# Moving a scan, a square and the splits of pooled rows on two vector engines of a hybrid encoder layer

## The chip, the cores and the metric

The kernel runs on one core of one Trainium2 chip. A core has a matrix engine (TensorE, PE in the profile; its weight loads are shown as PEld), a vector engine (VectorE, DVE), an activation engine (ScalarE, ACT), a general engine (GpSimd, POOL) and a queue for transfers (SyncE, SP). Each engine works through its own list of instructions in order, and semaphores tie the lists together. The metric is the device time of the whole kernel in microseconds, taken as the median of several runs.

## What is computed

One layer for 512 tokens of width 1024, all in fp32. The input is normalised and projected to the columns of three token mixers and of three gates; the mixers' results are projected, gated and added, projected once more and added to the input; a gated feed-forward block follows.

```
h = rms_norm(x);  u_pool, u_lru, q, k, v, g = split(h @ w_in)
y_pool[g] = (mean of the last w tokens of u_pool[g] - u_pool[g]) @ w_pool[g] * scale    w = 2, 4, 8, 16
y_lru     = scan h_t = a_t * h_(t-1) + b_t,   a, b from a conv and two block gates of u_lru
y_sb      = stick-breaking attention, 8 heads x 128; q and k are RMS-normed by head:
            q * rsqrt(mean(q^2)),  k * rsqrt(mean(k^2))
merged = sum over mixers of sigmoid(g_m) * (y_m @ w_branch[m])
x = x + merged @ w_out;   x = x + (silu(h2 @ w_fg) * (h2 @ w_fu)) @ w_fd
```

## The kernel before

**Products in three parts.** Every fp32 operand of a large matmul is split into a high part in a reduced format (float32r) and a low part, the rest. A product is then three matmuls: high by high, high by low, low by high (`mm3`). Weights come from HBM as 128x1024 tiles and are split on the chip by `split_w` (lines 131 to 141): ACT copies the tile to `whi` (L139), DVE subtracts that from the tile to give `wlo` (L140). Each of the two tags has three buffers, so the third tile ahead can be split only when PE is done with the oldest. A splitter's two instructions have a high priority (60 above their surroundings), and the weights are asked for some tiles ahead of their use.

**What sets the order.** The program is written as one stream of matmuls. Other work is put into lists of small functions: `bg` (background) and, during attention, `abg`. After each group of matmuls `tick()` takes one entry from `abg` and one from `bg` (two while `bg` has over eight entries), and what these functions write stands there in the program. A scheduler then places each engine's instructions by data and by priority. `tc.issue_after(i)` adds one more rule to what is written inside it: on the engine of `i` it stands behind `i`, with no other wait.

**v, k and q.** The projection for v, k and q (in this order, `VKQ`; t = 2, 1, 0) uses seven products per matrix instead of eight, in the order `11, 12, S2, S1, S3, S4, 22`. `tok_product` does one of them: two weight tiles, 12 matmuls of 512 columns each per tile, with the token blocks (names such as hT3h, hT3l) as the stationary operand and the weight tile as the moving one. Results gather in PSUM. `snap` copies a partial result from PSUM to a buffer `r` on ACT (L841, a high priority), `final` adds another partial result on DVE (L845) and puts `post` into `bg`. For q, `post` squares the block on ACT (L788), adds the squares up by head on DVE (L789) and stores the block by a transfer from POOL. For k, `post2` also scales the block by eight short ACT instructions (L807).

**The recurrence.** The RG-LRU part works in four chunks of 256 channels. Its last steps stand in `bg` behind v's product S3: the input of chunk 3, two scans of chunk 2 and two of chunk 3 (`lru_scan`, L711, one instruction per 128 channels), and the stores. They run beside v's product S4 and 22 and beside k's first products.

**Pooling and attention.** Behind the gates, four pool chunks are projected (`pool_chunk`, order 1, 0, 3, 2), two blocks `j` of 128 channels each. `evac_u` copies a block out of PSUM (ACT L975, tile `up`), `pool_mean` forms the running mean by scans and two more DVE instructions (L985, L986, L987, L989; for window 2 an add), and ends with `split_hl`: ACT copies the block to `p..h` (L932), DVE subtracts to get `p..l` (L933); the name p30h is the high part of chunk 3, block 0. `pool_back` multiplies the blocks by the chunk's small matrix (PSUM tile `pps`) one chunk later. Attention runs from `abg` beside this, a head every five ticks: `trans` transposes q and k on PE (PSUM tile `pq`, L1053), `scores` (L1086 to L1092), `wtrans` transposes the weights (PSUM tile `pw`, L1103) and splits them on ACT (`wth`, L1105, three instructions) and DVE (`wtl`, L1106, three instructions), `yout` multiplies by v. The PSUM tiles pq, pps, pw and py share three buffers, so PE can write the next pq only when the split of an earlier pw has read it.

**The branch products** of the recurrence follow (`ps_br`). Their operands yHH and yHL are loaded from DRAM by POOL (L1192) into the buffers that the normalised input had, once PE has left these. Weights and small tiles are loaded by SP.

Of the kernel before, what the change touches and what calls it, by code (L numbers as in the profile page):

```python
# [8 lines left out]
F32 = mybir.dt.float32  # L9
F32R = mybir.dt.float32r  # L10
BF16 = mybir.dt.bfloat16
AF = mybir.ActivationFunctionType
ALU = mybir.AluOpType
# [51 lines left out]
def layer_kernel(ctx: ExitStack, tc: tile.TileContext, x, xt, vecs, w_in, w_qkv7, w_gate7, w_pool, w_rg, w_ig,  # L65
                 w_branch, w_br7, w_out, w_fg, w_fu, w_fd, w_fd7, out):
    nc = tc.nc
    act = nc.scalar.activation
# [30 lines left out]
    def in_order(ap, b=H):  # L99
        w = ap.ndim == 3  # L100
        if b == H:
            return ap.rearrange("p w (b a) -> p w a b" if w else "p (b a) -> p a b", b=b)
        return ap.rearrange("p (c b a) -> p c a b", a=2, b=b)

    def two(ap, b=H):
        w = ap.ndim == 3
        if b == H:
            return ap.rearrange("p w (a b) -> p w a b" if w else "p (a b) -> p a b", b=b)
        return ap.rearrange("p (c a b) -> p c a b", a=2, b=b)
# [18 lines left out]
    def weight_tiles(nh, nl):  # L128
        return [wp.tile([P, 1024], F32R, tag=tag, name=n)
                for tag, n in (("whi", nh), ("wlo", nl))]  # L130

    def split_w(raw, shape, n):
        hi, lo = weight_tiles("whi" + n, "wlo" + n)
        if len(shape) == 3:
            hi, lo = (t.rearrange("p (a b) -> p a b", a=shape[1]) for t in (hi, lo))
        else:
            hi, lo = (t.rearrange("p (a b c) -> p a b c", a=shape[1], b=shape[2]) for t in (hi, lo))
        with tc.high_priority(60):
            act(hi, raw, AF.Copy)  # L139
            dve.tensor_tensor(lo, raw, hi.bitcast(F32), ALU.subtract)  # L140
        return hi, lo

    def add_direct(key, src, a, b):
# [291 lines left out]
    with ExitStack() as first:  # L435
# [271 lines left out]
        def lru_scan(c):  # L707
            t, s_ = lru[c]["t"], lru[c]["s"]
            h = lru[c]["i"]
            for j in range(2):  # L710
                dve.tensor_tensor_scan(h[:, j, :], t[:, j, :], s_[:, j, :], 0.0, ALU.mult, ALU.add)  # L711
            lru[c] = h
# [39 lines left out]
        def step(*fs):  # L752
            bg.append(lambda: [f() for f in fs])

        def of(f, c):
            return lambda: f(c)
# [27 lines left out]
        def post(t, i, j, r):  # L784
            if t < 2:
                sq = b4([2, 512], f"sq{t}{i}{j}")
                if t == 0:
                    act(sq, r, AF.Square)  # L788
                    dve.tensor_reduce(qss[:, 2 * j:2 * j + 2, 4 * i:4 * i + 4],  # L789
                                      sq.rearrange("p a (b d) -> p a b d", d=HD), AX.X, ALU.add)  # L790
                    store(t, i, j, r)
                    return
                s_ = cst.tile([P, 8], F32, tag="ssq", name=f"ssq{t}{i}{j}", bufs=2)
                act(sq, r, AF.Square)
                dve.tensor_reduce(s_, sq.rearrange("p a (b d) -> p (a b) d", d=HD), AX.X, ALU.add)
                dve.tensor_scalar(s_, s_, 1.0 / HD, EPS, ALU.mult, ALU.add)
                bg.append(lambda: post2(t, i, j, r, s_))
            if t == 2:
                store(t, i, j, r)
# [33 lines left out]
        for t in VKQ:  # L833
            ps = {}
            r = {}


            def snap(key, src):
                r[key] = b4([2, 512], f"r{t}{key[0]}{key[1]}")
                with tc.high_priority(EARLY):  # L840
                    act(two(r[key]), in_order(src), AF.Copy, scale=-1.0 if key[0] else 1.0)  # L841

            def final(key, src):
                v = two(r[key])
                dve.tensor_tensor(v, v, in_order(src), ALU.subtract if key[0] else ALU.add)  # L845
                bg.append(lambda t=t, key=key, v=r[key]: post(t, *key, v))

            def bank(nm):
                ps[nm] = pb.tile([P, 2, 512], F32, tag="mm", name=f"ps_q{t}{nm}")
                return ps[nm]  # L850

            for nm in ORDER:
                if nm in ("11", "12", "S1", "22"):
                    bank(nm)
                dst = {"S2": "11", "S3": "11", "S4": "S1"}.get(nm, nm)
                tok_product(t, nm, ps[dst], dst == nm)
                if nm == "11":
                    snap((0, 0), ps["11"])
                elif nm == "12":
                    final((0, 0), ps["12"])  # L860
                elif nm == "S2":
                    snap((0, 1), ps["11"])
                elif nm == "S1":
                    snap((1, 1), ps["S1"])
                elif nm == "S3":
                    final((1, 1), ps["11"])
                    snap((1, 0), ps["11"])
                elif nm == "S4":
                    final((0, 1), ps["S1"])
                else:  # L870
                    final((1, 0), ps["22"])
                if (t, nm) == (VKQ[0], "S3"):
                    for f, c in ((lru_input, 3), (lru_scan, 2), (lru_scan, 3), (lru_store, 2), (lru_store, 3)):
                        step(of(f, c))


        def gate_done(cc, j, t, ps):
# [51 lines left out]
    def split_hl(src, nm):  # L929
        h = slot_r(nm + "h")  # L930
        l = slot_r(nm + "l")
        act(h, src, AF.Copy)  # L932
        dve.tensor_tensor(l, src, h.bitcast(F32), ALU.subtract)  # L933
        return h, l

    with ExitStack() as mix:
# [41 lines left out]
        def pool_mean(g, j, u):  # L978
            w = 2 << g
            prev = slot(f"pw{g}{j}")  # L980
            if w == 2:
                dve.tensor_copy(prev[:, 0:1], u[:, 0:1])
                dve.tensor_tensor(prev[:, 1:], u[:, 1:], u[:, 0:S - 1], ALU.add)
            else:
                dve.tensor_tensor_scan(prev[:, 0:w], u[:, 0:w], ahead[:, 0:w], 0.0, ALU.add, ALU.add)  # L985
                dve.tensor_tensor_scan(prev[:, w:], u[:, w:], u[:, 0:S - w], prev[:, w - 1:w], ALU.add, ALU.subtract)  # L986
            dve.scalar_tensor_tensor(prev[:, 0:w - 1], prev[:, 0:w - 1], float(w),  # L987
                                     invpos[:, 0:w - 1], ALU.mult, ALU.mult)
            dve.scalar_tensor_tensor(u, prev, 1.0 / w, u, ALU.mult, ALU.subtract)  # L989
            pool_p.setdefault(g, []).append(split_hl(u, f"p{g}{j}"))  # L990

        def pool_back(g, j):
            wh, wl = pool_w[g]
# [12 lines left out]
        def queue_pool_back(g):  # L1006
            for j in range(2):
                bg.append(lambda j=j: pool_back(g, j))
            if g == POOL[1]:
                bg.append(lambda: load_pool_weights(1))  # L1010

        def pool_chunk(g):
            pss = chan_chunk(("pool", g), hn, 1)
            us = [evac_u(pss[j], f"up{g}{j}", g == POOL[3]) for j in range(2)]
            for j in range(2):
                bg.append(lambda j=j, u=us[j]: pool_mean(g, j, u))
            if g != POOL[0]:
                queue_pool_back(POOL[POOL.index(g) - 1])


        def gate_load(br, c):
# [710 lines left out]
```

## Time and profile before

| | us |
|---|---|
| median of 3 runs | 870.37 (870.13 to 870.64) |
| the profiled execution | 870.05 |
| its span in the trace | 868.3 |
| PE busy / weight loads busy | 859.3 / 789.9 |
| DVE busy | 736.4 |
| ACT busy | 522.3 |
| POOL busy | 91.0 |

The granted clock of TensorE was 1.00 over the whole span. The profiled execution is 0.32 us below the median of the runs and 1.75 us above its own span. Times in the trace are counted from the start of the span. In a row of a timeline the columns are start, busy time, engine, line, operation, output and inputs, shapes, count of instructions put together in the row, and in brackets the time that the engine stood idle just before, with what ended it. PE's matmuls are pipelined: in an undisturbed stretch one of 512 columns starts every 0.2155 us (162.60 to 162.82, 353.58 to 353.80), though each is listed with 0.38 us, so a stall is read from the starts: the distance of two starts less 0.2155.

### The profile page before, as it was taken

Reading aid. Unit: us, or ns where it says so; the run is one execution under the profiler, and the core shown is the slowest. Engines: PE = TensorE matmul, PEld = TensorE weight load, DVE = VectorE, ACT = ScalarE, POOL = GpSimd, SP = SyncE. Lnnn points to the kernel's source line nnn. Section 1 sums busy time; section 2 is a strip of 40 time slices with the busy share of each in tenths; the row PEclk is TensorE's granted clock in tenths of the full one; section 3 lists DMA queues with packets and bytes.
Section 4 is the critical chain, followed back from the end, with each engine's and each line's share of the span. In section 5 each row is a group of like instructions: output and inputs, shape, how many; then the busy total and the mean of one; then the engine's idle time right before and its main releaser. Section 6 shows DMA issues by size and latency. Waiting matters only on the chain.

```text
span 868.3 us, 14234 instructions
## 1 busy us (share of the span) xinstructions
PE 859.3 (99%) x5563; PEld 789.9 (91%) x5563; DVE 736.4 (85%) x937; ACT 522.3 (60%) x727; POOL 91.0 (10%) x130
## 2 busy tenths in 40 slices
PE   9999999999999999999999999999999999999998
PEld 7888878888899988889889998889999999999998
DVE  7899897998796698967898786699998888899974
ACT  6554989557866567555665545464555555755642
POOL 1110002232433101000001100000000000021200
PEclk9999999999999999999999999999999999999999
DMA  9586356899592776735736955345543433798913
GB/s 340 168 295 193 98 169 187 226 314 253 178 298 73 240 221 207 228 112 158 217 98 154 211 170 171 98 135 155 153 116 97 114 106 117 225 243 203 196 40 122
DMA packets 116643, 154.08 MB, mean 177 GB/s; under 512 B 8160, under 2 KB 90080, under 8 KB 116576
## 3 DMA queue, kind: packets, MB, share of 16 engines
q1 hardware_dynamic: 103904, 107.30, 38.5%
q0 software_dynamic: 12528, 45.62, 22.3%
q8 instruction: 43, 0.70, 0.3%
q10 hardware_dynamic: 144, 0.26, 0.1%
q14 instruction: 24, 0.20, 0.1%
HBM read 132.71 MB, written 18.87 MB: 175 GB/s over the span
## 4 chain that ended last, share of the span: by engine, by line
PE 56%; DVE 5%; ACT 2%; issue 1%; DMA 1%; SPq 0%; DVEq 0%; ACTq 0%
PE ps_y L313 11%; PE ps_x L313 8%; PE ps_dy L1651 6%; PE ps_dx L1651 5%; PE ps_bY L1276 2%; PE ps_br L305 2%; PE ps_br L304 2%; PE ps_br L306 2%; PE ps_bX L1276 2%; PE ps_out L304 1%; PE ps_out L305 1%; PE ps_out L306 1%; DVE wlo L140 1%; PE ps_fu L306 1%; PE ps_fu L304 1%; PE ps_fu L305 1%
## 5 line engine op out<-in xcount | busy, mean ns | idle before, releaser
L139 ACT ACTIVATE whi<-raw 128x1024 fp32r<-128x1024 f32 x69 | 72.8, 1056 | 72.7 <-PE ps_out L305 15.9
L140 DVE TENSOR_TENSOR wlo<-raw,whi 128x1024 fp32r<-128x1024 f32 x69 | 84.4, 1223 | 23.6 <-ACT whi L139 23.1
L140 DVE TENSOR_TENSOR wlo<-qw,whi 128x1024 fp32r<-128x1024 f32 x48 | 58.5, 1222 | 16.5 <-ACT whi L139 16.3
L139 ACT ACTIVATE whi<-qw 128x1024 fp32r<-128x1024 f32 x48 | 50.6, 1054 | 31.1 <-PE ps_q L828 15.6
L1437 ACT ACTIVATE wh_S<-w_S 128x1024 fp32r<-128x1024 f32 x36 | 38.3, 1063 | 30.3 <-PE ps_y L313 18.4
L1557 POOL DMA_DIRECT2D dw<-in_w_down_dram x20 | 16.9, 862 | 305.3 <-DMA dw<-in_w_down_dram 262.7
L1438 DVE TENSOR_TENSOR wl_S<-w_S,wh_S 128x1024 fp32r<-128x1024 f32 x36 | 43.9, 1222 | 3.3 <-ACT wh_S L1437 3.3
L1437 ACT ACTIVATE wh<-w 128x1024 fp32r<-128x1024 f32 x27 | 28.6, 1059 | 28.1 <-PE ps_x L313 9.1
L1438 DVE TENSOR_TENSOR wl<-w,wh 128x1024 fp32r<-128x1024 f32 x27 | 33.0, 1223 | 8.2 <-ACT wh L1437 8.2
L1437 ACT ACTIVATE whdS<-dw 128x1024 fp32r<-128x1024 f32 x20 | 21.2, 1058 | 20.7 <-PE ps_dy L1651 10.6
L1090 DVE TENSOR_TENSOR_SCAN E<-K,ahead 128x512 f32<-128x512 f32 (+3 forms) x32 | 25.4, 816 | 4.3 <-ACT K L1086 4.3
L1438 DVE TENSOR_TENSOR wldS<-dw,whdS 128x1024 fp32r<-128x1024 f32 x20 | 24.3, 1223 | 5.0 <-ACT whdS L1437 5.0
L304 PE MATMUL ps_lru<-HH,whi 128*128 128x512 f32 x64 | 24.6, 384 | 0.0
L304 PE MATMUL ps_br<-yph,whi 128*128 128x512 f32 x64 | 24.5, 383 | 0.0
L304 PE MATMUL ps_br<-yHH,whi 128*128 128x512 f32 x64 | 24.5, 383 | 0.0
L304 PE MATMUL ps_pool<-HH,whi 128*128 128x512 f32 x64 | 24.5, 383 | 0.0
L305 PE MATMUL ps_br<-yHL,whi 128*128 128x512 f32 x64 | 24.4, 381 | 0.0
L304 PE MATMUL ps_gate<-HH,whi 128*128 128x512 f32 x64 | 24.4, 381 | 0.0
L306 PE MATMUL ps_pool<-HH,wlo 128*128 128x512 f32 x64 | 24.3, 379 | 0.0
L305 PE MATMUL ps_lru<-HL,whi 128*128 128x512 f32 x64 | 24.3, 379 | 0.0
L305 PE MATMUL ps_br<-ypl,whi 128*128 128x512 f32 x64 | 24.3, 379 | 0.0
L306 PE MATMUL ps_gate<-HH,wlo 128*128 128x512 f32 x64 | 24.3, 379 | 0.0
(740 smaller groups left out, 3439.8 us busy)
## 6 DMA issues: line engine op xcount, KB each, us to landing
raw<-in_w_in_dram SPq DMA_DIRECT2D x31, 512.0 KB, 5.5
qw<-in_w_qkv_dram SPq DMA_DIRECT2D x24, 512.0 KB, 8.6
dw<-in_w_down_dram POOLq DMA_DIRECT2D x20, 512.0 KB, 8.4
w<-in_w_ffn_gate_dram SPq DMA_DIRECT2D x36, 256.0 KB, 3.6
w<-in_w_ffn_up_dram SPq DMA_DIRECT2D x36, 256.0 KB, 4.5
raw<-in_w_branch_dram SPq DMA_DIRECT2D x16, 512.0 KB, 3.5
qw<-in_w_qkv_dram POOLq DMA_DIRECT2D x12, 512.0 KB, 8.3
qd<-r POOLq DMA_DIRECT2D x12, 512.0 KB, 7.4
```

The source lines that it names most:

```text
L139: act(hi, raw, AF.Copy)
L140: dve.tensor_tensor(lo, raw, hi.bitcast(F32), ALU.subtract)
L304: nc.tensor.matmul(ps, lh, rh, start=start, stop=False, skip_group_check=skip)
L305: nc.tensor.matmul(ps, lh, rl, start=False, stop=False, skip_group_check=skip)
L306: nc.tensor.matmul(ps, ll, rh, start=False, stop=stop, skip_group_check=skip)
L313: nc.tensor.matmul(o, a_[a][:, w, k, :], il2(b_[b][:, k, :]), start=first and n == k == 0, stop=last and n == 2 and k == 3, skip_group_che ...
L1090: dve.tensor_tensor_scan(E[:, c0:c0 + n][:, ::-1], K[:, c0 + 1:c0 + n + 1][:, ::-1], ahead[:, S - n:][:, ::-1], 0.0, ALU.mult, ALU.add)
L1276: nc.tensor.matmul(o, ah[x_][:, w, k, :], il2(b[k][y_]), start=first_ and n == k == 0, stop=n == 2 and k == 3, skip_group_check=True)
L1437: act(h, src, AF.Copy)
L1438: dve.tensor_tensor(l, src, h.bitcast(F32), ALU.subtract)
L1557: nc.gpsimd.dma_start(buf[n], dsrc(nm, n), accum_op=ALU.add)
L1651: nc.tensor.matmul(o, a_[a][:, w, k0 + k, :], il2(b_[b][:, k, :]), start=first and i == k == 0, stop=last and i == 2 and k == nk - 1, skip ...
```

## The change

Three groups of instructions are put at other places in the program; none is removed or added.

The low-part subtractions are kept in a list `los`. The scans of the last recurrence chunk (chunk 3) are written inside `issue_after(los[-5])`, which is the subtraction for the second weight tile of v's product S3 (wlo33 in the order below; the number counts the weight tiles).

On DVE in v's product S3, before. wlo32 and wlo33 are the low parts of S3's two weight tiles, wlo34 and wlo35 those of S4's; li2 and li3 are the scans of chunks 2 and 3 (the scan instruction is printed under the name of the form it shares):

```order
L140 TENSOR_TENSOR wlo32_1470<-qw2110_1200,whi32_1469 128x1024
L711 SCALAR_TENSOR_TENSOR li2_898<-lt2_1118,ls2_1249 128x512 x2
L711 SCALAR_TENSOR_TENSOR li3_1083<-lt3_1224,ls3_1251 128x512
L140 TENSOR_TENSOR wlo33_1486<-qw2111_1202,whi33_1485 128x1024
L711 SCALAR_TENSOR_TENSOR li3_1083<-lt3_1224,ls3_1251 128x512
L140 TENSOR_TENSOR wlo34_1509<-qw2120_1204,whi34_1508 128x1024
L140 TENSOR_TENSOR wlo35_1526<-qw2121_1206,whi35_1525 128x1024
```

The same place after the change:

```order
L142 TENSOR_TENSOR wlo32_1470<-qw2110_1200,whi32_1469 128x1024
L713 SCALAR_TENSOR_TENSOR li2_898<-lt2_1118,ls2_1249 128x512 x2
L142 TENSOR_TENSOR wlo33_1486<-qw2111_1202,whi33_1485 128x1024
L713 SCALAR_TENSOR_TENSOR li3_1083<-lt3_1224,ls3_1251 128x512 x2
L142 TENSOR_TENSOR wlo34_1509<-qw2120_1204,whi34_1508 128x1024
L142 TENSOR_TENSOR wlo35_1526<-qw2121_1206,whi35_1525 128x1024
```

wlo33 now stands behind the two scans of chunk 2 alone; both scans of chunk 3 come between it and wlo34.

For q, the result of the first block, (0,0), is not put into `bg` by `final` any more. A step queued behind product S2 does its `post`, behind the ACT instruction of the snapshot of block (0,1).

On ACT at q's products 12 and S2, before. krs10 scales k's block (1,0), whi60 and whi61 are the high parts of weight tiles 60 and 61, sq000 is the square of q's block (0,0), r001 the snapshot of block (0,1):

```order
L807 ACTIVATE r110_1852<-r110_1852,krs10_1989 128x128 x5
L139 ACTIVATE whi60_2105<-qw0110_1795 128x1024
L807 ACTIVATE r110_1852<-r110_1852,krs10_1989 128x128 x3
L788 ACTIVATE sq000_2067<-r000_2027 128x1024
L841 ACTIVATE r001_2102<-ps_q011_1973 128x1024
L139 ACTIVATE whi61_2121<-qw0111_1797 128x1024
L841 ACTIVATE r011_2139<-ps_q0S1_2104 128x1024
```

The same place after the change:

```order
L809 ACTIVATE r110_1852<-r110_1852,krs10_1989 128x128 x5
L843 ACTIVATE r001_2098<-ps_q011_1973 128x1024
L141 ACTIVATE whi60_2101<-qw0110_1795 128x1024
L809 ACTIVATE r110_1852<-r110_1852,krs10_1989 128x128 x3
L141 ACTIVATE whi61_2121<-qw0111_1797 128x1024
L790 ACTIVATE sq000_2105<-r000_2027 128x1024
L843 ACTIVATE r011_2139<-ps_q0S1_2100 128x1024
```

The snapshot r001 went from behind the square to ahead of whi60, and the square from ahead of whi61 to behind it. On DVE the sum of these squares (L789) went with it, from ahead of wlo61 to behind it.

`pool_mean` no longer splits its block but returns the split as a function. Block 0 of a chunk is split after the mean of block 1, and block 1 in a later step: together with the first `pool_back` of the chunk before, or in a step of its own for the first chunk.

On ACT at the transposed weights of head 1 (pw1, wth), before. p20h is the high part of pooled chunk 2, block 0, wph the high part of the small pool matrices, whi91 a weight tile of the branch products:

```order
L1002 ACTIVATE yph01_3319<-pps01_3312,vt_72 128x512
L968 ACTIVATE wph10_3365<-rawp1_3363 128x512
L968 ACTIVATE wph11_3369<-rawp1_3363 128x512
L932 ACTIVATE p20h_3425<-up20_3323 128x512
L139 ACTIVATE whi91_3431<-raw91_3429 128x1024
L1105 ACTIVATE wth0_2732<-pw1_0_3385 128x512
L1105 ACTIVATE wth1_2733<-pw1_1_3392 128x384
```

The same place after the change:

```order
L981 ACTIVATE wph11_3369<-rawp1_3363 128x512
L141 ACTIVATE whi91_3427<-raw91_3425 128x1024
L1128 ACTIVATE wth0_2732<-pw1_0_3385 128x512
L1128 ACTIVATE wth1_2733<-pw1_1_3392 128x384
L1128 ACTIVATE wth2_2734<-pw1_2_3398 128x384
L1109 ACTIVATE K1_2741<-z2_1_3404,qrs_110 128x128
L1110 ACTIVATE A2_1_3411<-z2_1_3404,qrs_110 128x128
L1109 ACTIVATE K1_2741<-z2_1_3404,qrs_110 128x384
L1110 ACTIVATE A2_1_3411<-z2_1_3404,qrs_110 128x384
L1079 ACTIVATE qkh30_3448<-pq30_3443,qg_113 128x512
L1079 ACTIVATE qkh31_3457<-pq31_3452,vt_72 128x512
L141 ACTIVATE whi92_3537<-raw92_3535 128x1024
L945 ACTIVATE p20h_3466<-up20_3323 128x512
```

p20h went from ahead of whi91 and of wth to behind whi92. In the same way p30h went from ahead of the wth of head 0 to behind the qkh of head 2 and p31h, p21h and the blocks of chunks 1 and 0 went later; the low parts on DVE went with them. The orders on PE and POOL are as before. On SP one weight load of the branch products stands behind an attention load that it stood ahead of.

```diff
--- before.py
+++ after.py
@@ -129,6 +129,8 @@
         return [wp.tile([P, 1024], F32R, tag=tag, name=n)
                 for tag, n in (("whi", nh), ("wlo", nl))]
 
+    los = []
+
     def split_w(raw, shape, n):
         hi, lo = weight_tiles("whi" + n, "wlo" + n)
         if len(shape) == 3:
@@ -137,7 +139,7 @@
             hi, lo = (t.rearrange("p (a b c) -> p a b c", a=shape[1], b=shape[2]) for t in (hi, lo))
         with tc.high_priority(60):
             act(hi, raw, AF.Copy)
-            dve.tensor_tensor(lo, raw, hi.bitcast(F32), ALU.subtract)
+            los.append(dve.tensor_tensor(lo, raw, hi.bitcast(F32), ALU.subtract).ins)
         return hi, lo
 
     def add_direct(key, src, a, b):
@@ -838,12 +840,17 @@
             def snap(key, src):
                 r[key] = b4([2, 512], f"r{t}{key[0]}{key[1]}")
                 with tc.high_priority(EARLY):
-                    act(two(r[key]), in_order(src), AF.Copy, scale=-1.0 if key[0] else 1.0)
+                    state["snap"] = act(two(r[key]), in_order(src), AF.Copy, scale=-1.0 if key[0] else 1.0)
+
+            def post_behind(key):
+                with tc.issue_after(state["snap"].ins):
+                    post(t, *key, r[key])
 
             def final(key, src):
                 v = two(r[key])
                 dve.tensor_tensor(v, v, in_order(src), ALU.subtract if key[0] else ALU.add)
-                bg.append(lambda t=t, key=key, v=r[key]: post(t, *key, v))
+                if (t, key) != (0, (0, 0)):
+                    bg.append(lambda t=t, key=key, v=r[key]: post(t, *key, v))
 
             def bank(nm):
                 ps[nm] = pb.tile([P, 2, 512], F32, tag="mm", name=f"ps_q{t}{nm}")
@@ -860,6 +867,8 @@
                     final((0, 0), ps["12"])
                 elif nm == "S2":
                     snap((0, 1), ps["11"])
+                    if t == 0:
+                        step(lambda: post_behind((0, 0)))
                 elif nm == "S1":
                     snap((1, 1), ps["S1"])
                 elif nm == "S3":
@@ -870,8 +879,12 @@
                 else:
                     final((1, 0), ps["22"])
                 if (t, nm) == (VKQ[0], "S3"):
-                    for f, c in ((lru_input, 3), (lru_scan, 2), (lru_scan, 3), (lru_store, 2), (lru_store, 3)):
-                        step(of(f, c))
+                    def last_scan():
+                        with tc.issue_after(los[-5]):
+                            lru_scan(3)
+
+                    step(of(lru_input, 3)), step(of(lru_scan, 2)), step(last_scan)
+                    step(of(lru_store, 2)), step(of(lru_store, 3))
 
 
         def gate_done(cc, j, t, ps):
@@ -987,7 +1000,7 @@
             dve.scalar_tensor_tensor(prev[:, 0:w - 1], prev[:, 0:w - 1], float(w),
                                      invpos[:, 0:w - 1], ALU.mult, ALU.mult)
             dve.scalar_tensor_tensor(u, prev, 1.0 / w, u, ALU.mult, ALU.subtract)
-            pool_p.setdefault(g, []).append(split_hl(u, f"p{g}{j}"))
+            return lambda: pool_p.setdefault(g, []).append(split_hl(u, f"p{g}{j}"))
 
         def pool_back(g, j):
             wh, wl = pool_w[g]
@@ -1012,10 +1025,20 @@
         def pool_chunk(g):
             pss = chan_chunk(("pool", g), hn, 1)
             us = [evac_u(pss[j], f"up{g}{j}", g == POOL[3]) for j in range(2)]
-            for j in range(2):
-                bg.append(lambda j=j, u=us[j]: pool_mean(g, j, u))
+            split = []
+
+            def mean(j):
+                split.append(pool_mean(g, j, us[j]))
+                if j:
+                    split.pop(0)()
+
+            bg.extend([lambda: mean(0), lambda: mean(1)])
             if g != POOL[0]:
                 queue_pool_back(POOL[POOL.index(g) - 1])
+                back = bg[-3 if POOL.index(g) == 2 else -2]
+                bg[bg.index(back)] = lambda: (back(), split.pop(0)())
+            else:
+                bg.append(lambda: split.pop(0)())
 
 
         def gate_load(br, c):
```

## The prediction

> **What bounds the kernel now.** I read the page first, then the starts of PE's matmuls, then what ended PE's waits, and then each place by engine.
>
> ```profile
> span 868.3 us, 14234 instructions
> PE 859.3 (99%) x5563; PEld 789.9 (91%) x5563; DVE 736.4 (85%) x937; ACT 522.3 (60%) x727; POOL 91.0 (10%) x130
> ```
>
> PE is busy for 859.3 of 868.3 us. The change takes no matmul away, so it can only win what PE stands still. PE's own waits, by what ended them:
>
> ```profile
> PE ps_q L828 <- DVE wlo L140: 1.1, 2, 0.8
> PE pq L1053 <- DVE wtl L1106: 1.0, 3, 0.7
> PE ps_q L828 <- ACT r L841: 0.4, 1, 0.4
> ```
>
> The columns are the sum of the waits, their number and the longest. These three rows are what the change can aim at. They understate the loss, since a matmul here is listed longer than its distance to the next; I take the distance of two starts less 0.2155 us throughout.
>
> **Place A, v's product S3.** DVE, then PE:
>
> ```profile
> 159.42 3.45 DVE L711 TENSOR_TENSOR_SCAN li<-lt,ls 128x512 f32<-128x512 f32 x3
> 162.78 1.20 DVE L140 TENSOR_TENSOR wlo<-qw,whi 128x1024 fp32r<-128x1024 f32 x1
> 163.90 1.22 DVE L711 TENSOR_TENSOR_SCAN li<-lt,ls 128x512 f32<-128x512 f32 x1
> 165.03 2.34 DVE L140 TENSOR_TENSOR wlo<-qw,whi 128x1024 fp32r<-128x1024 f32 x2
> ...
> 162.82 0.38 PE L828 MATMUL ps_q<-whi,hT3h 128*128 128x512 f32 x1
> 164.04 0.48 PE L828 MATMUL ps_q<-wlo,hT3h 128*128 128x512 f32 x1 [0.84 <-DVE wlo L140]
> 164.36 0.38 PE L828 MATMUL ps_q<-whi,hT3l 128*128 128x512 f32 x1
> ...
> 166.74 0.38 PE L828 MATMUL ps_q2S<-wlo,HH 128*128 128x512 f32 x1
> ```
>
> PE could use wlo33 at 162.82 + 0.22 = 163.04, but it ends at 163.98 behind three scans. Lost: 164.04 − 162.82 − 0.22 = 1.01, and 0.10 more at the next start (164.36 − 164.04 − 0.22): 1.11. After the change two scans stand ahead of wlo33; a scan takes about 1.12 of DVE's time (162.78 − 159.42 over three), so wlo33 starts at 161.67 and ends at 162.87: in time by 0.17. But nothing leaves DVE. Its row is gapless from 159.42 to the end of wlo34 at 165.03 + 1.20 = 166.23, and all four scans still stand ahead of wlo34, so wlo34 ends at 166.23 as before. PE used it at 166.74; without the stall it asks 1.11 sooner, at 165.63. It then waits until about 166.28: 0.65, plus 0.10 for the restart. The wait is moved to the next product and shortened: A is worth 1.11 − 0.75 = 0.36. The bounds are 0.25 (DVE's handover 0.1 slower) and 1.11 (wlo34 not late).
>
> **Place B, q's product S2.** ACT, DVE, PE:
>
> ```profile
> 230.64 1.04 ACT L139 ACTIVATE whi<-qw 128x1024 fp32r<-128x1024 f32 x1
> 231.59 0.97 ACT L807 ACTIVATE r<-r,krs 128x128 f32<-128x128 f32 x3
> 232.46 1.04 ACT L788 ACTIVATE sq<-r 128x1024 f32<-128x1024 f32 x1
> 233.41 1.00 ACT L841 ACTIVATE r<-ps_q 128x1024 f32<-128x1024 f32 x1
> ...
> 231.71 1.23 DVE L140 TENSOR_TENSOR wlo<-qw,whi 128x1024 fp32r<-128x1024 f32 x1 [1.45 <-ACT whi L139]
> ...
> 233.64 0.38 PE L828 MATMUL ps_q0S<-whi,hT1l 128*128 128x512 f32 x1
> 234.46 0.48 PE L828 MATMUL ps_q<-whi,hT3h 128*128 128x512 f32 x1 [0.44 <-ACT r L841]
> ```
>
> PE waits to add into the PSUM tile that the snapshot still reads: 234.46 − 233.64 − 0.22 = 0.60, and 0.10 for the restart: 0.70. The new order is snapshot, whi60, three scalings, whi61, square. The snapshot takes whi60's place at 230.64 and is over 2.8 us sooner than now. whi60 goes 0.90 later, to 231.54, and wlo60 on DVE from 231.71 to about 232.61, ending at 233.84; PE's need is the second matmul at 233.86 + 0.22 = 234.07. It fits by 0.2. DVE's wait of 1.45 for whi60 shows that nothing else is in its way. The square and its sum on DVE go behind whi61 and wlo61. Their reader is the scale of q in the gate stretch, over 30 us on; the block's store goes along, POOL being busy for 91 of 868 us. B is worth 0.70; the lower bound is 0.35, if PE gets A's 0.36 early and ACT doesn't move with it, so that wlo60 is late by 0.15 and a restart.
>
> Both stalls cost 0.10 beyond the wait, because the start behind the late matmul is late too. The Trainium skill, "TensorE: Matmul & The Clock Gate", Part 2, says that PE pulls weight loads ahead of running matmuls; if that reached past a waiting matmul, there would be no restart, B would be worth 0.60 and the whole sum 1.9 instead of 2.0. The trace speaks against it here: 164.04 to 164.36 is 0.32, not 0.22.
>
> **Place C, two splits of pooled rows.** First p30, beside head 0:
>
> ```profile
> 330.94 0.63 ACT L932 ACTIVATE p30h<-up 128x512 fp32r<-128x512 f32 x1 [2.64 <-DVE up L989]
> 331.47 1.34 ACT L1105 ACTIVATE wth<-pw 128x512 fp32r<-128x512 f32 x3
> ...
> 331.60 0.69 DVE L933 TENSOR_TENSOR p30l<-up,p30h 128x512 fp32r<-128x512 f32 x1 [0.76 <-ACT p30h L932]
> 332.21 1.61 DVE L1106 TENSOR_TENSOR wtl<-pw,wth 128x512 fp32r<-128x512 f32 x3
> ...
> 328.09 1.26 PE L1103 MATMUL pw<-idn,A 128*128 128x128 f32 x10
> 332.38 0.38 PE L306 MATMUL ps_pool<-HH,wlo 128*128 128x512 f32 x1
> 332.94 1.12 PE L1053 MATMUL pq<-idn,at 128*128 128x128 f32 x8 [0.18 <-DVE wtl L1106]
> ```
>
> PE's transposes pw are over at 329.35, yet ACT stands 2.64 for the pooled mean with p30h at the head of its list and wth behind it. PE then waits for the first wtl to free a PSUM buffer: 332.94 − 332.38 − 0.22 = 0.34. With p30h behind, wth starts at about 329.4 and the first wtl follows the mean at 330.84, ending near 331.5, 1.1 before PE's need at 332.60. C1 is worth 0.34. Then p20 beside head 1:
>
> ```profile
> 351.77 0.63 ACT L932 ACTIVATE p20h<-up 128x512 fp32r<-128x512 f32 x1 [4.00 <-DVE up L989]
> ...
> 353.38 1.23 DVE L140 TENSOR_TENSOR wlo<-raw,whi 128x1024 fp32r<-128x1024 f32 x1 [0.25 <-ACT whi L139]
> 354.52 1.61 DVE L1106 TENSOR_TENSOR wtl<-pw,wth 128x512 fp32r<-128x512 f32 x3
> ...
> 354.23 0.38 PE L306 MATMUL ps_br<-yHH,wlo 128*128 128x512 f32 x1
> 355.26 1.12 PE L1053 MATMUL pq<-idn,at 128*128 128x128 f32 x8 [0.66 <-DVE wtl L1106]
> ```
>
> Here PE loses 355.26 − 354.23 − 0.22 = 0.81. With whi91 (1.04, like whi60) and wth (1.34, like head 0's) no longer behind p20h, most of them fits into ACT's idle 4.00 us; wlo91 starts when the mean is done (351.77) and ends at 353.0, the first wtl at about 353.5, 0.9 before PE's need at 354.45. C2 is worth 0.81.
>
> What is late next? Each displaced split costs ACT 0.54 and DVE 0.6 elsewhere. p20h now stands behind whi92 and also waits for the second mean, which is over at 364.60 (365.30 less the wait of 0.70, below); the low parts then come some 2 to 3 us later than p21l did:
>
> ```profile
> 365.30 0.69 DVE L933 TENSOR_TENSOR p21l<-up,p21h 128x512 fp32r<-128x512 f32 x1 [0.70 <-ACT p21h L932]
> 370.23 0.38 PE L305 MATMUL pps<-p21l,wph 128*128 128x512 f32 x1
> ```
>
> p21l ended at 365.99 and PE read it at 370.23, a slack of 4.2; behind a scan of 1.22, a subtraction of 0.69 and a wait of 0.76 more it keeps 1.5. I cost it at nothing; its cover is that slack, and without it each us of lateness would be one of PE.
>
> **The y loads, a term against.** At the head of the branch products PE waits once more, for a transfer:
>
> ```profile
> 352.86 0.38 PE L304 MATMUL ps_br<-yHH,whi 128*128 128x512 f32 x1
> 353.26 0.48 PE L305 MATMUL ps_br<-yHL,whi 128*128 128x512 f32 x1
> 344.32 0.56 POOL L1192 DMA_DIRECT2D yHL<-ydl  x1
> DMA to landing us min/median/max: 4.0/6.7/9.4
> ```
>
> From the last issue at 344.32 to PE's start at 353.26 are 8.9 us, within the slowest landing of 9.4; PE loses 0.18 and 0.10 for the restart, 0.29 unrounded. POOL's issue follows PE, which frees the buffers, and so comes earlier with it. The weight loads that share the transfer engines follow DVE's wlo, and DVE loses the wait of 0.76 (above) while PE gains 0.34 there: up to 0.42 sooner against PE. So this term lies between +0.29 (the wait gone) and −0.42; I take −0.2.
>
> **The sum.** 0.36 + 0.70 + 0.34 + 0.81 − 0.2 = 2.0. The profiled execution would go from 870.05 to 868.05. The median of the runs stands 0.32 above it, and the same distance gives 868.37; I say 868.3. That is −0.24%; what a measurement of this kernel can tell from no change, 0.2%, is 1.74 us, so faster means under 868.63 and slower over 872.11. Behind these places PE keeps its lead if the others have room:
>
> ```profile
> 380.00:440.00 60.00, 59.56 (x329) 52.93 (x328) 47.67 (x78) 34.80 (x69) 1.73 (x2) 1.00 0.60 180
> ```
>
> From 380 to 440 DVE (third busy time, 47.67 of 60) has 12 us free, so a lead of 2 is carried.
>
> **The rivals.** First, the gains of A and B are swallowed before C. A's wait goes whole to wlo34 or wlo35 (0), and B brings 0.35 or less, because wlo60 has only 0.2. Then 0.35 + 0.34 + 0.81 − 0.2 = 1.3: 869.1. For it speaks DVE's gapless row in A; against it that wlo34's slack of 0.5 (166.23 to 166.74) is real room. This would be "within 0.2%".
>
> Second, the whole of A is won (wlo34 not late, because scans that don't interrupt wlo33 run closer) and the y wait goes too: 1.11 + 0.70 + 0.34 + 0.81 + 0.29 = 3.25: 867.1.
>
> Third, slower: the y loads land later. POOL's four issues (0.56 each) go 1.4 sooner into another stretch of DVE's work, and if each has to stand until a DVE operation (0.69 to 1.23, as p21l and wlo91) is over, the last lands 2.8 to 4.9 later, against 2.2 won elsewhere: 871.0 to 873.1. It decides from 2.2 us of lateness, and over 0.2% from 3.9. Against it, POOL's issue at 344.32 took 0.56, as long as DVE's work beside it was under way:
>
> ```profile
> 343.88 0.75 DVE L1003 SCALAR_TENSOR_TENSOR ypl<-pps,vt,yph 128x512 fp32r<-128x512 f32 x1
> ```
>
> The Trainium skill, "SBUF — State Buffer", section "SBUF: two separate sides", warns of this: a transfer issued from POOL's queue can starve while DVE holds the port that the two share. Here the trace disagrees for these operations, by the 0.56 beside one of 0.75.
>
> **How the numbers follow.** The forecast, all four gains at about their sizes: 0.53, with its own range 867.8 to 868.6. More than that, the second rival or part of it: 0.05. The first rival, A or B or both without yield: 0.28. The third, or another wait that I don't see in the displaced splits: 0.14. So faster 0.58, same 0.28, slower 0.14. The range goes from 867.4, between forecast and second rival, to 870.2, past the first rival; what it leaves out is most of the third and the end of the second.
>
> **What would show it.** Right: no start over 0.3 apart at 162 to 165, but one of about 0.87 near 165.6 with wlo as its releaser; none near 233 for r; none for wtl at 331 and 353. Wrong: A's new wait over 1.0 or none; wlo60 ending after PE's need; a pps matmul that waits for p20l or p21l; yHL's wait over 0.6. A lead that shows at 360 and is gone at 500 would be a stage behind that doesn't follow PE.

## The result, and the profile after

| | before | after |
|---|---|---|
| median, us | 870.37 (869.89 to 871.27, 11 runs) | 867.85 (867.52 to 869.35, 11 runs) |
| ratio | | 0.9972 (95% interval 0.9963 to 0.9980) |
| span of the profiled execution, us | 868.3 | 866.0 |
| PE / DVE / ACT busy, us | 859.3 / 736.4 / 522.3 | 858.7 / 735.7 / 522.9 |

The kernel is 2.5 us faster, 0.28%; the upper end of the interval lies just at the 0.2% from which the prediction speaks of faster. In a second group of runs (below) the changed kernel measured 868.11 beside 870.30, a ratio of 0.9974 (0.9965 to 0.9984). The head of the page after, and three rows of PE's own waits for engines (sum, times, longest):

```profile
span 866.0 us, 14235 instructions
PE 858.7 (99%) x5563; PEld 789.7 (91%) x5563; DVE 735.7 (85%) x937; ACT 522.9 (60%) x727; POOL 90.8 (10%) x130
```

```profile
PE ps_q2S L830 <- DVE wlo L142: 0.5, 1, 0.5
PE ps_q L830 <- DVE wlo L142: 0.2, 1, 0.2
PE pq L1076 <- DVE wtl L1129: 0.2, 1, 0.2
```

The row for the snapshot is gone, that for wtl shrank from 1.0 to 0.2 (the rest is a later head, near 427), and what is left of the wait for wlo at place A is in `ps_q2S` now, the next product. The 0.2 in `ps_q` is another wait, near 145, which stood before too. The engines do the same work; only PE's idle starts went.

**Place A.** DVE, then PE, in the timeline after:

```profile
159.61 2.33 DVE L713 TENSOR_TENSOR_SCAN li<-lt,ls 128x512 f32<-128x512 f32 x2
161.86 1.20 DVE L142 TENSOR_TENSOR wlo<-qw,whi 128x1024 fp32r<-128x1024 f32 x1
162.98 2.33 DVE L713 TENSOR_TENSOR_SCAN li<-lt,ls 128x512 f32<-128x512 f32 x2
165.23 2.33 DVE L142 TENSOR_TENSOR wlo<-qw,whi 128x1024 fp32r<-128x1024 f32 x2
...
165.60 0.38 PE L830 MATMUL ps_q2S<-whi,HH 128*128 128x512 f32 x1
166.48 0.48 PE L830 MATMUL ps_q2S<-wlo,HH 128*128 128x512 f32 x1 [0.50 <-DVE wlo L142]
166.80 0.38 PE L830 MATMUL ps_q2S<-whi,HL 128*128 128x512 f32 x1
```

wlo33 is over at 163.06 and stops nobody. wlo34 ends at 166.43, 0.20 later than before only because this execution's first matmuls came 0.2 later. PE asks for it at 165.82 and gets it at 166.48: 0.66 and 0.10 for the restart, 0.77 in all (unrounded) where 1.11 was.

**Place B.** ACT, DVE, PE:

```profile
230.50 1.00 ACT L843 ACTIVATE r<-ps_q 128x1024 f32<-128x1024 f32 x1
231.40 1.04 ACT L141 ACTIVATE whi<-qw 128x1024 fp32r<-128x1024 f32 x1
...
232.48 1.23 DVE L142 TENSOR_TENSOR wlo<-qw,whi 128x1024 fp32r<-128x1024 f32 x1 [2.35 <-ACT whi L141]
...
233.71 0.38 PE L830 MATMUL ps_q<-whi,hT3h 128*128 128x512 f32 x1
233.93 0.38 PE L830 MATMUL ps_q<-wlo,hT3h 128*128 128x512 f32 x1
```

The snapshot ends 2.2 us before PE adds into its tile. wlo60 ends at 233.71, 0.22 before its first use at 233.93. PE loses nothing here.

**Place C and the y loads.** PE at the two pq and at the first yHL of the second weight tile:

```profile
331.52 0.38 PE L308 MATMUL ps_pool<-HH,wlo 128*128 128x512 f32 x1
331.74 1.04 PE L1076 MATMUL pq<-idn,at 128*128 128x128 f32 x8
...
351.57 0.38 PE L306 MATMUL ps_br<-yHH,whi 128*128 128x512 f32 x1
351.88 0.48 PE L307 MATMUL ps_br<-yHL,whi 128*128 128x512 f32 x1
...
352.85 0.38 PE L308 MATMUL ps_br<-yHH,wlo 128*128 128x512 f32 x1
353.06 1.04 PE L1076 MATMUL pq<-idn,at 128*128 128x128 f32 x8
```

Both pq start 0.22 after the matmul ahead of them: nothing is lost. The wait for yHL is 0.10 with 0.10 for its restart, 0.20 instead of 0.29. SP's transfers behind the last y load, before and then after:

```profile
345.80 4.17 SPq L146 DMA_DIRECT2D raw<-in_w_branch_dram  x2
343.56 7.50 SPq L148 DMA_DIRECT2D raw<-in_w_branch_dram  x3
```

The next weight load was issued 1.48 us after the last y load before (344.32) and 0.52 after it now (343.04). It came 0.96 sooner against the y loads, where the prediction allowed for 0.42.

By starts, then: A +0.34, B +0.71, C +0.35 and +0.82, y +0.09, and −0.20 at the very first matmuls, which wait for the input: 2.1. The last part of the program starts 2.30 us earlier (the ps_x matmul just ahead of the ps_y that waits for tx, in the feed-forward block, at 602.10 before and 599.80 after), and the span is 2.3 shorter; the remaining 0.2 lies in starts of less than 0.1 each.

### The profile page after: what moved, and what is told of

Same layout as the page of the kernel before. It is cut to its first block, busy times and chain, and to the rows that moved or that the text cites. A ratio compares the mean times of both kernels' runs of the same rounds, so it can differ in the third digit from the quotient of the medians.

```text
span 866.0 us, 14235 instructions
## 1 busy us (share of the span) xinstructions
PE 858.7 (99%) x5563; PEld 789.7 (91%) x5563; DVE 735.7 (85%) x937; ACT 522.9 (60%) x727; POOL 90.8 (10%) x130
## 4 chain that ended last, share of the span: by engine, by line
PE 88%; DVE 5%; ACT 4%; issue 1%; DMA 1%; SPq 0%; DVEq 0%; ACTq 0%
PE ps_y L315 11%; PE ps_x L315 8%; PE ps_q L830 7%; PE ps_dy L1674 6%; PE ps_dx L1674 5%; PE ps_br L307 3%; PE ps_br L306 3%; PE ps_br L308 3%; PE ps_bY L1299 2%; PE ps_gy L315 2%; PE ps_gate L733 2%; DVE wlo L142 2%; PE ps_bX L1299 2%; PE ps_gx L315 2%; PE ps_pool L307 2%; PE ps_pool L306 2%
## 5 line engine op out<-in xcount | busy, mean ns | idle before, releaser
L308 PE MATMUL ps_lru<-HH,wlo 128*128 128x512 f32 x64 | 24.3, 379 | 0.0
L307 PE MATMUL ps_gate<-HL,whi 128*128 128x512 f32 x64 | 24.3, 379 | 0.0
```

Of the source, the lines that this page charges most:

```text
L307: nc.tensor.matmul(ps, lh, rl, start=False, stop=False, skip_group_check=skip)
L308: nc.tensor.matmul(ps, ll, rh, start=False, stop=stop, skip_group_check=skip)
```

## The experiments

Each theory is the one of the prediction unless it is named otherwise. Times at places are sums of starts beyond 0.2155 us, restart included, from one profiled execution each; PE's first matmuls, which wait for the input, lost between 0.1 us less and 2.7 us more than in the profile before, so places are compared and not spans. The three parts and the first run of the section behind them were measured on one chip, the others on a second one; the kernel before had 870.42 and 870.30 there.

### One part at a time

Part A alone:

```diff
+            los.append(dve.tensor_tensor(lo, raw, hi.bitcast(F32), ALU.subtract).ins)
...
+                    def last_scan():
+                        with tc.issue_after(los[-5]):
+                            lru_scan(3)
```

(The lines that these replace are left out.)

> Only the scans of chunk 3 are moved behind wlo33, nothing else. Theory (the wait is moved to the next weight tile): the start that is 1.22 us apart at 162.8 goes, and one of about 0.88 appears at the first matmul of product S4 that uses wlo34, because four scans still stand ahead of wlo34; 1.11 - 0.77 = 0.34 us won, 870.0 us. Rival 1 (DVE's order doesn't matter there, something else held PE): 1.1 us won, or none. Rival 2 (the lead is lost to DVE later): the wait at wlo34 as said, but further starts over 0.3 apart between 170 and 230, and the span unchanged within 0.1 us.

Measured: 870.24 us against 870.42, ratio 0.9996 (0.9986 to 1.0005). PE at product S4:

```profile
168.09 0.38 PE L830 MATMUL ps_q2S<-whi,HH 128*128 128x512 f32 x1
168.97 0.48 PE L830 MATMUL ps_q2S<-wlo,HH 128*128 128x512 f32 x1 [0.50 <-DVE wlo L142]
```

The 1.22 is gone and 0.88 stands at the next product, as the theory said: 0.77 lost in place of 1.11. The time alone can't show 0.34 us; its interval holds both 0.34 and 0. The rows show it, and rule out rival 1. There is no new start over 0.3 between 170 and 230, which rules out rival 2.

Part B alone:

```diff
+            def post_behind(key):
+                with tc.issue_after(state["snap"].ins):
+                    post(t, *key, r[key])
...
                     snap((0, 1), ps["11"])
+                    if t == 0:
+                        step(lambda: post_behind((0, 0)))
```

(The other lines of this part are those of the change.)

> Only the post of q's block (0,0) is put behind the snapshot of block (0,1). Theory: the start 0.82 us apart at 233.6 and its restart go, 0.71 us won, 869.7 us; wlo60 ends about 0.2 us before PE needs it. Rival (the short way from whi60 to wlo60 now ends last): wlo60 ends after the need, a new wait with DVE wlo as its releaser, 0.35 us won or less. All else as in the kernel before.

Measured: 869.94 against 870.42, ratio 0.9991 (0.9981 to 1.0000). At q's S2 nothing is lost:

```profile
234.34 0.38 PE L828 MATMUL ps_q0S<-whi,hT1l 128*128 128x512 f32 x1
234.56 0.38 PE L828 MATMUL ps_q<-whi,hT3h 128*128 128x512 f32 x1
...
354.06 0.38 PE L306 MATMUL ps_br<-yHH,wlo 128*128 128x512 f32 x1
355.21 0.33 PE L1060 MATMUL pq<-idn,at 128*128 128x128 f32 x1 [0.77 <-DVE wtl L1113]
```

The 0.71 is won in full at its place and no wlo is late. At the untouched place C the wait for wtl is longer than before: 355.21 − 354.06 − 0.22 = 0.93 instead of 0.82. But yHL, five matmuls earlier, cost 0.17 here instead of 0.29. The two add up to 1.10 here, 1.10 with part A alone (0.35 + 0.75) and 1.11 before (0.29 + 0.82): wtl's end sets when PE goes on, and what PE waits for yHL it doesn't wait for wtl. A wait for yHL is thus hidden as long as wtl is late, by an estimate from these sums up to about 1.1 us of it, and stands bare once part C is made.

Part C alone:

```diff
-            pool_p.setdefault(g, []).append(split_hl(u, f"p{g}{j}"))
+            return lambda: pool_p.setdefault(g, []).append(split_hl(u, f"p{g}{j}"))
```

(with the queueing in `pool_chunk` as in the change)

> Only the splits of the pooled rows are moved. Theory: the starts 0.56 apart at 332.4 and 1.03 apart at 354.2 go, 0.35 + 0.82 = 1.17 us won, 869.2 us; the wait for yHL between them stays within 0.1 of its 0.29, because the loads are issued when PE leaves the buffers and so move with PE. Rival (the weight loads come forward against the y loads): yHL's wait grows to 0.5 or more, under 0.95 us won. Second rival (the displaced splits are late): a wait of a pps matmul for p20l or p21l near 368.

Measured: 869.51 against 870.42, ratio 0.9988 (0.9979 to 0.9998). Both waits for wtl are gone (0.35 + 0.82). The wait for yHL grew:

```profile
353.19 0.38 PE L304 MATMUL ps_br<-yHH,whi 128*128 128x512 f32 x1
353.93 0.48 PE L305 MATMUL ps_br<-yHL,whi 128*128 128x512 f32 x1 [0.36 <-DMA yHL<-ydl]
...
352.20 1.61 DVE L1116 TENSOR_TENSOR wtl<-pw,wth 128x512 fp32r<-128x512 f32 x3
```

0.52 and 0.10, 0.63 in all, 0.34 more than before. On this the theory failed and the rival gave the right size (0.83 won at the places). No pps matmul waited for a displaced split. The first wtl starts at 352.20, 2.9 us before PE's next pq at 355.11 (0.34 of this is PE's own longer wait for yHL); before, it started 0.07 after PE could have gone on (354.52 against 354.45). The two instructions moved away, p20h and p20l, take about 0.53 and 0.61 by the starts of p30h, p30l and what followed them, so most of the shift is the wait at the head of ACT's list that is gone, and not their own time. Whether the order or the single execution made the y wait longer, this run alone can't tell.

The three parts alone give 0.18, 0.48 and 0.91 us by their medians, 1.6 together; each interval is about 0.8 us to either side, so the missing 0.9 to the 2.5 of the whole is no finding by itself.

### What is left of the wait at A, and what yHL's wait hangs on

The changed kernel with both scans of chunk 3 one subtraction further back:

```diff
                     def last_scan():
-                        with tc.issue_after(los[-5]):
+                        with tc.issue_after(los[-4]):
                             lru_scan(3)
```

On DVE this moves wlo34 ahead of the two scans and nothing else on any engine.

> The changed kernel with both scans of chunk 3 put behind wlo34 instead of wlo33. Theory (four scans ahead of wlo34 are the whole of what is left of the wait at place A): the 0.88 us start at 165.6 and its restart go, 0.77 us more than in the changed kernel, 867.1 us; the tightest later low part, wlo39 with 0.77 us of slack in the changed kernel, is then just in time. Rival (DVE has no free time until 170, so the wait moves on once more): a new wait at wlo35, wlo36 or wlo39 of 0.3 to 0.8 us, 867.4 to 867.9 us.

Measured: 869.02 against 870.42, ratio 0.9979 (0.9967 to 0.9991), with single runs from 867.03 to 871.84, a wider spread than any kernel here. In its profile place A loses nothing, but waits stand elsewhere: 1.78 us from 246 to 248, where a weight of the gates landed late,

```profile
244.67 1.22 DVE L214 TENSOR_TENSOR qs<-qw,qw 128x1024 f32<-128x1024 f32 x1 [3.22 <-DMA qw<-in_w_gate_dram]
```

1.14 for yHL at 353, and three starts between 502 and 511 that leave PE 1.6 later than before. The order of instructions at these places is that of the changed kernel, so the two kernels were run once more side by side, on the second chip. First the changed kernel:

> The changed kernel once more, beside the others of this group. Theory: 867.9 us again, the wait at wlo34 of 0.77, none at the snapshot and at the two wtl, and a wait for yHL that scatters from execution to execution between 0.1 and 1.1 us, since it hangs on when a transfer lands and not on the order. Rival (the wait for yHL is set by the order): 0.20 us again, within 0.05.

Measured: 868.11 against 870.30, ratio 0.9974 (0.9965 to 0.9984). The same kernel as in the first profile, with 0.77 at wlo34 again, now waits for yHL by 1.14 and 0.10, 1.24 in all, a little above the range expected, where it had waited 0.20:

```profile
351.66 0.38 PE L306 MATMUL ps_br<-yHH,whi 128*128 128x512 f32 x1
353.01 0.48 PE L307 MATMUL ps_br<-yHL,whi 128*128 128x512 f32 x1 [0.98 <-DMA yHL<-ydl]
```

So this wait scatters by a microsecond with an unchanged order, and the 0.34 that it grew by in the run of part C lies within that scatter. That the order adds nothing is not shown by this: in the three profiles without part C it was 0.17 to 0.35, in the seven with it 0.12 to 1.24, and SP's weight load follows the y loads sooner with part C. Then the kernel with wlo34 ahead of the scans:

> The changed kernel with both scans of chunk 3 behind wlo34, once more, beside the changed kernel. Theory: the 0.77 at wlo34 is won in every execution, 867.1 us, and the waits that took it back in the first profile (a gate weight that landed late at 244, yHL at 353) are those of one execution. Rival (PE's larger lead runs into transfers that do not come sooner): the wait at 246 again, 867.5 to 868.5 us.

Measured: 867.60 us beside 868.11, ratio to before 0.9965 (0.9954 to 0.9977). DVE and PE at A:

```profile
161.75 2.33 DVE L142 TENSOR_TENSOR wlo<-qw,whi 128x1024 fp32r<-128x1024 f32 x2
164.00 2.33 DVE L713 TENSOR_TENSOR_SCAN li<-lt,ls 128x512 f32<-128x512 f32 x2
166.25 1.19 DVE L142 TENSOR_TENSOR wlo<-qw,whi 128x1024 fp32r<-128x1024 f32 x1
...
165.49 0.38 PE L830 MATMUL ps_q2S<-whi,HH 128*128 128x512 f32 x1
165.70 0.38 PE L830 MATMUL ps_q2S<-wlo,HH 128*128 128x512 f32 x1
...
177.43 1.22 DVE L142 TENSOR_TENSOR wlo<-qw,whi 128x1024 fp32r<-128x1024 f32 x1
178.71 0.48 PE L830 MATMUL ps_q<-wlo,HH 128*128 128x512 f32 x1
179.03 0.38 PE L830 MATMUL ps_q<-whi,HL 128*128 128x512 f32 x1
```

No start is late at A: the whole 0.77 is won at its place, which shows that the two scans of chunk 3 ahead of wlo34 made all that was left of A. But most of it doesn't last. At the first use of a low part near 179, 187, 223 and 228 PE now loses 0.10 to 0.17 each, restart included, 0.56 together; the low part ended 0.06 earlier each time (178.65 for the start at 178.71). The changed kernel lost nothing at these four places. At 245 PE's lead over the changed kernel is 0.2, counted from the first matmuls, and the first profile shows the same 0.2. So the rival named for the first run of this kernel holds in small pieces: the wait at A moves on once more, to DVE's next low parts. The larger waits at 246 and above 502 of the first profile don't return; yHL waits (0.67), and 0.54 is lost near 791 to 794, two of its starts waiting for a low part of the down projection's weights. In the medians this kernel is 0.5 us ahead; the two intervals overlap, so that it beats the changed one is not shown by its times, and the lead of 0.2 doesn't account for 0.5.

### More lead, taken from another place

PE's longest wait, 1.71 us near 121 (xcl, the low part of the recurrence chunk's input), is untouched by the change. On top of the kernel above, two instructions were put behind xcl on DVE:

```diff
-                dve.scalar_tensor_tensor(st["i"], st["i"], 1.0, xc, ALU.add, ALU.mult)
+                with tc.issue_after(state["xcl"].ins): dve.scalar_tensor_tensor(st["i"], st["i"], 1.0, xc, ALU.add, ALU.mult)
...
-            dve.scalar_tensor_tensor(s_, e, 1.0, s_, ALU.add, ALU.mult)
+            with tc.issue_after(state["xcl"].ins): dve.scalar_tensor_tensor(s_, e, 1.0, s_, ALU.add, ALU.mult)
```

> As the one above, and the low part of the last recurrence chunk's input (xcl, for which PE waits 1.6 us near 121) put ahead of a product of chunk 2 and of an input product of chunk 1 on DVE. Theory: 1.1 us less at 121, as DVE reaches xcl one operation of 1.14 sooner; 866.0 us if the lead survives the transfers at 228 to 250. Rival (the lead is lost to the next transfers or to the scans of chunk 2, which now stand two places on): 867 us or more.

Measured: 867.75 us, ratio to before 0.9967 (0.9955 to 0.9980): no faster than the kernel without it. The wait at 121 did shrink by 1.0, and three others came up:

```profile
120.96 0.48 PE L660 MATMUL lg<-xcl,lwh 64*128 64x512 f32 x2 [0.34 <-DVE xcl L650]
...
143.95 0.48 PE L830 MATMUL ps_q<-wlo,HH 128*128 128x512 f32 x1 [0.51 <-DVE wlo L142]
...
147.36 0.48 PE L830 MATMUL ps_q<-wlo,HH 128*128 128x512 f32 x1 [0.55 <-DVE wlo L142]
...
160.94 0.48 PE L830 MATMUL ps_q<-wlo,hT3h 128*128 128x512 f32 x1 [0.36 <-DVE wlo L142]
```

They cost 0.78, 0.82 and 0.63, where the kernel above lost 0.51 at the first and nothing at the others: 1.7 given back for 1.0 won. The scheduler had also rearranged DVE behind the moved instructions (one of the scans of chunk 2 stood ahead of wlo31, the other ahead of wlo32), and a few instructions on ACT, so this run doesn't tell how much was the lead and how much the order. But DVE runs without a gap from 141.54 to 163.16 there, so a PE that comes sooner finds it no sooner done. The rival of this run holds in its time and in that the lead was lost. Of its reasons only the scans of chunk 2 can stand behind the third wait; the first two came before any of these scans.

### POOL's issues beside copies on DVE

```diff
         act(h, src, AF.Copy)
+        for _ in range(8 if nm == "p31" else 0):
+            dve.tensor_copy(l, src)
```

> The changed kernel with eight more copies of a pooled block (fp32 to fp32r, 128x512, on DVE) ahead of p31l, so that DVE copies without a break while POOL issues the last four y loads. The third rival of the prediction (DVE holds POOL's issues up): each issue takes 0.3 us or more longer than 0.53 to 0.57, the last is over 1 us later behind the first than 1.56, and yHL's wait grows to 1 us or more. Theory (DVE's work doesn't touch them): issues of 0.53 to 0.57, the last 1.56 behind the first, yHL's wait within its scatter.

Measured, one run: 868.87 us. POOL and DVE:

```profile
341.70 0.59 POOL L1217 DMA_DIRECT2D yHL<-ydl  x1 [7.33 <-PE ps_pool L308]
342.28 1.07 POOL L1217 DMA_DIRECT2D yHH<-ydh  x2
343.32 0.56 POOL L1217 DMA_DIRECT2D yHL<-ydl  x1
...
340.83 2.26 DVE L947 CAST p31l<-up 128x512 fp32r<-128x512 f32 x5
```

The copies did not run without a break: five of them, until 343.09, cover the first two issues and half of the third, a wlo covers the rest, and the other three copies come later. The first issue took 0.59 instead of 0.53, the others the same as ever, and the last was issued 1.62 behind the first instead of 1.56. yHL's wait was 1.07: that is the size that this rival named, but it is also within the scatter (0.20 to 1.24 for the unchanged order), so the wait decides nothing. By the issues, the third rival of the prediction doesn't hold here, in one run. The Trainium skill's warning ("SBUF — State Buffer", "SBUF: two separate sides") that DVE can keep a transfer of POOL's queue from being set up is about DVE's two-port modes, with fp32 copies inside SBUF as its example. The operation that the prediction set against it, ypl, reads PSUM and is not such a copy, so it doesn't speak against the page; the copies here are nearer to it, though the trace doesn't show the mode they ran in. Beside them the issues grew by 0.06 us at most.

## Why the prediction was right, point by point

The forecast was 868.3 (867.4 to 870.2), faster; measured 867.85.

- **A, 0.36.** Measured 0.34 in the profile after and in the part alone. The step that wlo34 keeps its end because four scans still stand ahead of it was the right one: with them behind it, the remaining 0.77 went.
- **B, 0.70.** Measured 0.71. wlo60's margin, worked out as 0.2, was 0.22.
- **C, 0.34 and 0.81.** Measured 0.35 and 0.82. That the head of ACT's list, and not its load, held wth showed in the part alone, where both waits went and the first wtl of head 1 came 2.9 us ahead of the need.
- **The displaced splits, at nothing.** p21l ended 2.0 us before PE read it, where 1.5 was worked out; no pps matmul waited in any run.

```profile
365.26 0.67 DVE L946 TENSOR_TENSOR p21l<-up,p21h 128x512 fp32r<-128x512 f32 x1
367.95 0.38 PE L307 MATMUL pps<-p21l,wph 128*128 128x512 f32 x1
```

- **The y loads, −0.2 between +0.29 and −0.42.** This is the term that was mis-sized. The first profile gave +0.09, the second of the same kernel −0.95, with a wait of 1.24 that the prediction had named, from 0.6 on, as a sign of being wrong. The row before, 0.29, was one draw from a scatter of a microsecond, and bounds worked out from it with DVE's and PE's shifts were too narrow; the shift itself was 0.96 and not 0.42. It was also half hidden: what PE waited for yHL came off its wait for wtl, so that the two together, 1.11 before, are what part C can win, less what yHL then costs bare (0.20 or 1.24). The order sets when the loads are issued (1.28 us sooner with PE 1.29 us sooner, in the first profile after), but not by itself when they land.
- **The restart of 0.10**, taken from rows against a reading of the rule in the Trainium skill, "TensorE: Matmul & The Clock Gate", Part 2, stood behind the new wait too (166.48 to 166.80) and behind the waits for wlo and yHL of the other runs.
- **The lead is carried.** 2.30 us stood at the feed-forward block; no later wait grew.
- **The first rival (A and B without yield)** did not hold: A's wait did move to wlo34, but by 0.77 and not whole, and B's 0.71 came in full. **The second rival** needed wlo34 in time, which it was not. **The third** is spoken against by the issues in the run of copies.

With A, B and C right to 0.02 each, the profiled execution came 0.29 us under the 868.05 of the sum, and that is the y term: +0.09 in place of −0.2. (The 0.20 lost at the first matmuls and the 0.2 won in small starts cancel.) The median then stood 0.09 above its profiled execution instead of the 0.32 taken from the kernel before. That the y term came out near its forecast in this execution is luck: the second profile of the same kernel, 868.89, lies above the 868.63 that the prediction set as its bound for faster, and the medians, 867.85 and 868.11, lie below it.

## What to carry to other kernels

On an engine that works in order, moving one item ahead of a wait helps until the next item that is due: before counting a stall as won, work out when the next due item ends with the same work still ahead of it, here 0.77 of 1.11. And count again when that one is moved too: of the 0.77, 0.2 was left eighty microseconds on. An item that waits for another engine should not stand ahead of one that is ready and whose result frees a buffer; the place to look for is a long idle time ahead of a short instruction, such as 4.00 us ahead of a copy of 0.63. A wait for a transfer that is seen once has no size yet: take a second profile of the same kernel before giving it a sign in a sum, and expect a lead to be given back where an engine runs without gaps.

## What the runs showed that was not expected

The wait for yHL, at the same order of all instructions, was 0.20 and 1.24 us in two executions of the changed kernel, and 1.14 and 0.67 in two of the kernel with wlo34 ahead; the kernel with xcl moved, whose POOL and SP have the same order, lost 0.12. The time from the last issue to PE's start was 8.8 us in the first profile after, 8.9 before, 9.3 with part C alone, 9.8 in the first profile with wlo34 ahead, 9.3 in its second, and 9.9 in the second after. In the five executions of the first sentence SP issued its next weight load 0.51 to 0.53 us after the last y load, so the moment of that issue doesn't make the difference between them. What makes the transfers land later in one execution than in another stays open, and so does whether the sooner weight load of part C makes the wait longer in the mean; weight loads from SP were not moved by themselves.
